# A decoder layer on one core: two quads with sums instead of three, a ring given back by halves, a new order of output and attention steps

## The chip, the cores and the metric

The kernel runs on one core of one Trainium2 chip. TensorE (PE) multiplies, VectorE (DVE) and ScalarE (ACT) work element by element, GpSimd (POOL) does next to nothing here, and SyncE (SP) issues the transfers. Times are microseconds. What counts is the device time of one execution; the figure given is the median of several.

## The reference

The program computes one layer of a decoder on x of 256 tokens by 2048 channels (f32), with RMSNorm ahead of each block:

```
x = x + 1/2 * SwiGLU_1(RMSNorm(x))
h = RMSNorm(x); h @ W_in -> conv B, C, x | pool p | q, k, v | 3 gates
x = x + W_out( sig(gA)*Wa(B*conv3(C*x)) + sig(gB)*Wb(pool(p)) + sig(gC)*Wc(attention(q,k,v)) )
x = x + 1/2 * SwiGLU_2(RMSNorm(x))
out = RMSNorm(x)
swiglu(h, w_in, w_out): a, b = split(h @ w_in); (silu(a) * b) @ w_out
```

The hidden width of each SwiGLU (FFN) is 5632. Attention has 8 heads of 128 over the 256 tokens, causal with a linear distance penalty.

## The kernel before

**Products.** Weights come from memory as f32 blocks of 128 x 512. ACT copies a block to a rounded `whi` (`high`, L236) and DVE forms the rest `wlo` (`low`, L240); the activations are kept in the same two parts. Every product is three matmuls of 512 columns: high x high, low x high, high x low (`three`). One transfer brings four blocks (1 MB, `emit_dma`, three buffers); one transfer is one *step*.

**Pairs.** In an FFN, 512 columns of a and the matching 512 of b are a *pair* (11 per FFN), computed in 8 quads of 256 input channels. In a plain quad ("P") four weight blocks meet four activation forms in 8 products. In a quad with sums ("S") a scheme with 7 products is used: DVE adds blocks in place (`block_sums`, L245 to L248), three blocks are used directly (kind "A") and the four summed blocks as kind "T". An S quad so has 21 matmuls and a P quad 24. `PATTERN` gives the kinds of a pair's quads; the first pair of each FFN is all P. The sums accumulate in eight PSUM banks K1 to K7 and K22. After the last S quad three early steps (`e1`, `e2`, `e3`) combine banks, one per half-step; after the last quad `evac` adds the rest, takes the sigmoid and multiplies: silu(a) * b as a token-major tile `gt`. Its two halves are transposed on PE later (`turn`), and split into gh and gl (L474, L475): the left side of the output products.

**Parts.** `PARTS = (3, 3, 2, 3)`: after so many pairs come their output chunks: four column chunks j, each of as many steps as the part has pairs (24 matmuls per step), added into the residual `xr` by `ev_o` (L500). With C steps next, the two `turn`s of the last pair are due 4 and 5 half-steps after its end. A step whose left side doesn't exist yet pops the waiting side work by force.

**Ring.** `whi` and `wlo` are a ring of `RING` blocks. `prepare(n)` takes blocks for the first kind of step n+1 and, where step n has sums, for its T blocks, and emits `high`, `block_sums` and `low`; `need(n)` says how many blocks must be free. `prepare_ahead` runs at each step's start as far as blocks are free; `release(n)` gives a step's blocks back when the step is emitted. Since each engine takes its instructions in the order in which they are emitted, this order decides who stands behind whom. From 12 steps before the end of the first FFN to the end of the mixer, blocks from `LEND` on are lent out as tiles ("units"), so the mixer has a ring of `LEND` blocks.

**Side work.** `later` puts closures into a queue with due half-steps; `lazy` ones (attention: `scores`, `transp`, `pv` for each head in turn) are popped one every two half-steps. The pool branch needs pool weights: at step `n_ffn1 - 2` they are issued (L867) and, right there, split by ACT and DVE (L869, L870).

**Start.** x0raw (x transposed) comes in four pieces j; `forms_xT` makes the forms of quads 2j and 2j+1. At steps 0, 2 and 4 it stands ahead of `prepare_ahead`. At steps 0 and 1 the last two pieces of x0raw and the two row blocks of x (1 MB each) are issued.

Of the kernel before, what the change touches and what calls it, by code (L numbers as in the profile page):

```python
# [26 lines left out]
PARTS = (3, 3, 2, 3)  # L27
PATTERN = "SPSPSPPP"
UNITS = 20
RAW_BUFS = 3  # L30
LOOK_DMA = 3
RING = 18
LEND = 10
DELAY = 3
# [8 lines left out]

K1, K2, K3, K4, K6, K7, K5, K22 = range(8)
NF = 8
# [13 lines left out]
def f32(ap):  # L59
    return ap.bitcast(F32)  # L60


@with_exitstack
def hybrid_trunk(ctx: ExitStack, tc: tile.TileContext, x, xT, wst, vecs, poolw, fnorm, consts, out):
# [76 lines left out]
    def wide(b):  # L141

        return bank[:, b:b + 2].rearrange("p b (k s) -> p (b k) s", s=S)

    def side_psum():

        at = steps[cur[0]]
        if at["kind"] != "C":
            assert not at["set"]["sums"]
            return wide(K6)  # L150
        return wide(take(4, 6) if at["far"] else 6)
# [22 lines left out]
    def pair(forms, pattern, early, evac):  # L174
# [102 lines left out]

    def prepare_ahead():
        while prepared[0] < len(steps) and need(prepared[0]) <= len(free):
            prepare(prepared[0])  # L280
            prepared[0] += 1

    def release(n):
        for a in steps[n]["items"]:
            free.extend(parts_t.pop((n, a)))
        reclaim()
        raw_t.pop(n, None)

# [131 lines left out]


    def in_set(n, xs, c, gs, pattern):

        t = {}
        pb = lambda k: bank[:, k]

        def e1():
            t["pu"], t["vw"] = tok_tile("pu"), tok_tile("vw")
            nc.scalar.activation(t["pu"][:, 0], pb(K1), AF.Copy)
            nc.vector.tensor_sub(t["pu"][:, 1], t["pu"][:, 0], pb(K6))  # L430

        def e2():
            u = t["pu"][:, 1:2].to_broadcast((P, 2, CH))
            nc.vector.tensor_add(t["vw"], bank[:, K7:K7 + 2], u)  # L434

        def e3():
            nc.vector.tensor_add(t["pu"][:, 1], t["vw"][:, 0], pb(K5))

        def evac():
            r = norm[n]  # L440
            if "S" in pattern:
                pu, vw = t["pu"], t["vw"]
                a = pu[:, 0], vw[:, 0]
                b = vw[:, 1], pu[:, 1]
# [4 lines left out]
            else:  # L449
                a, b = (pb(K2), pb(K4)), (pb(K3), pb(K22))  # L450
# [8 lines left out]
            if "S" in pattern:  # L459
                drop(t["pu"], t["vw"])  # L460
            if c == 10:
# [26 lines left out]
    def ffn(n, xs, after, first):  # L488
# [3 lines left out]
        for p, cnt in enumerate(PARTS):  # L492
# [82 lines left out]
    def ev_v(c):  # L575
# [8 lines left out]
        return ev  # L584

    def attention(h):
        slope = 2.0 ** (-(8.0 / H) * (h + 1))
# [46 lines left out]

        lazy.extend([scores, transp, pv])

# [181 lines left out]
    nc.scalar.activation(junk[:, :NT], mhalf, AF.Sigmoid)  # L818
    ps = wide(K6)
    for i in range(WARM):  # L820
# [41 lines left out]
    for n, g in enumerate(steps):  # L862
        cur[0] = n
        if n == n_ffn1 - 2:
            for c in range(2):
                raw = unit("pw", F32, (P, 2, 2, S))
                nc.sync.dma_start(raw, poolw[:, 2 * c:2 * c + 2])  # L867
                pw[c] = unit("pwh", F32R, (P, 2, 2, S)), unit("pwl", F32R, (P, 2, 2, S))
                nc.scalar.activation(pw[c][0], raw, AF.Copy)  # L869
                nc.vector.tensor_sub(pw[c][1], raw, f32(pw[c][0]))  # L870
                drop(raw)
            mx["inv"] = unit("inv", F32)
            nc.sync.dma_start(mx["inv"].rearrange("p g s -> p (g s)"), consts[:, C_INV:C_END])
# [22 lines left out]
        if n < tail_from:  # L896
            prepare_ahead()
        for half in range(2):
# [5 lines left out]
            while True:  # L904
                try:
# [153 lines left out]
```

## Time and profile before

| | |
|---|---|
| runs | 2343.77, 2345.73, 2346.03 us; median 2345.73 |
| profiled execution | 2341.46 us, its span 2339.7 us |
| PE busy | 2271.6 us, 97%, 10145 matmuls and transposes |
| DVE busy | 1542.9 us, 66% |
| ACT busy | 1050.7 us, 45% |
| DMA | 438.61 MB, mean 187 GB/s |
| mean granted clock of PE | 0.992 |

The shares are means over stages with different limits. Busy time of PE counts matmuls from start to modelled end, which overlap; the time between two starts is what a matmul costs. A granted clock of 1.00 is 2.4 GHz, 0.50 is 1.2 GHz.

### The profile page before, as it was taken

Reading aid. Unit: us, or ns where it says so; the run is one execution under the profiler, and the core shown is the slowest. Engines: PE = TensorE matmul, PEld = TensorE weight load, DVE = VectorE, ACT = ScalarE, POOL = GpSimd, SP = SyncE. Lnnn points to the kernel's source line nnn. Section 1 sums busy time; section 2 is a strip of 40 time slices with the busy share of each in tenths; the row PEclk is TensorE's granted clock in tenths of the full one; section 3 lists DMA queues with packets and bytes.
Section 4 is the critical chain, followed back from the end, with each engine's and each line's share of the span. In section 5 each row is a group of like instructions: output and inputs, shape, how many; then the busy total and the mean of one; then the engine's idle time right before and its main releaser. Section 6 shows DMA issues by size and latency. Waiting matters only on the chain.

```text
span 2339.7 us, 24296 instructions
## 1 busy us (share of the span) xinstructions
PE 2271.6 (97%) x10145; PEld 1866.5 (80%) x10145; DVE 1542.9 (66%) x1327; ACT 1050.7 (45%) x857; POOL 3.7 (0%) x9
## 2 busy tenths in 40 slices
PE   8999999999998999999999999999999999999998
PEld 6778788878877888888778888888878788878877
DVE  6976885867974565544544545556876885867975
ACT  6544453444444444444544334344544453444543
POOL 0000000000000000000000000000000000000000
PEclk9999999999999999999999999999999999999999
DMA  7464554455454545554445555545454554455453
GB/s 275 180 218 177 202 212 162 180 202 194 180 192 158 181 163 187 190 181 179 162 167 190 185 195 191 185 180 200 178 217 179 199 209 168 180 199 193 184 203 121
DMA packets 63470, 438.61 MB, mean 187 GB/s; under 512 B 7168, under 2 KB 7936, under 8 KB 11264
## 3 DMA queue, kind: packets, MB, share of 16 engines
q1 hardware_dynamic: 63360, 437.06, 51.2%
q8 instruction: 79, 1.29, 0.2%
q14 instruction: 31, 0.25, 0.0%
HBM read 434.94 MB, written 2.10 MB: 187 GB/s over the span
## 4 chain that ended last, share of the span: by engine, by line
PE 75%; DVE 17%; ACT 4%; issue 3%; DMA 1%; SPq 0%; POOLq 0%; ACTq 0%; DVEq 0%
PE bank L310 49%; PE bank L299 24%; DVE wlo L240 9%; ACT whi L236 3%; DVE gt L456 1%; PE bank L377 1%; DVE raw L246 1%; DVE raw L247 1%; DVE raw L245 1%; DVE vw L434 1%; DVE gl L475 0%; DMA pw<-poolw_dram 0%; DMA x0raw<-xT_dram 0%; DVE pu L445 0%; DVE pu L448 0%
## 5 line engine op out<-in xcount | busy, mean ns | idle before, releaser
L240 DVE TENSOR_TENSOR wlo<-raw,whi 128x2048 fp32r<-128x2048 f32 (+2 forms) x483 | 1031.0, 2157 | 650.3 <-ACT whi L236 649.0
L236 ACT ACTIVATE whi<-raw 128x2048 fp32r<-128x2048 f32 (+2 forms) x483 | 865.4, 1807 | 974.4 <-PE bank L310 501.9
L299 PE MATMUL bank<-whi,fhl 128*128 128x512 f32 x1760 | 563.0, 393 | 5.1 <-ACT whi L236 5.1
L299 PEld LDWEIGHTS bank<-whi,fhl 128*128 128x128 f32 x1760 | 332.2, 189 | 73.7 <-ACT whi L236 5.6
L299 PE MATMUL bank<-wlo,fhl 128*128 128x512 f32 x880 | 344.4, 391 | 1.6 <-DVE wlo L240 1.5
L310 PE MATMUL bank<-whi 128*128 128x512 f32 x752 | 297.5, 396 | 6.0 <-ACT whi L236 6.0
L310 PE MATMUL bank<-wlo,whi 128*128 128x512 f32 x752 | 294.6, 392 | 3.2 <-DVE wlo L240 3.1
L310 PE MATMUL bank<-whi,wlo 128*128 128x512 f32 x752 | 294.2, 391 | 1.3 <-DVE wlo L475 1.3
L310 PE MATMUL bank<-whi,gl 128*128 128x512 f32 (+1 forms) x684 | 267.4, 391 | 10.1 <-DVE gl L475 10.1
L310 PE MATMUL bank<-whi,gh 128*128 128x512 f32 (+1 forms) x684 | 267.8, 391 | 3.3 <-ACT gh L474 3.3
L310 PE MATMUL bank<-wlo,gh 128*128 128x512 f32 (+1 forms) x684 | 266.0, 389 | 0.0
L299 PE MATMUL bank<-wlo,fh 128*128 128x512 f32 x468 | 184.1, 393 | 18.5 <-DVE wlo L240 18.5
L299 PEld LDWEIGHTS bank<-wlo,fhl 128*128 128x128 f32 x880 | 166.1, 189 | 36.2 <-DVE wlo L240 2.5
L299 PE MATMUL bank<-whi,fh 128*128 128x512 f32 x468 | 183.3, 392 | 1.9 <-ACT whi L236 1.6
L299 PE MATMUL bank<-whi,fl 128*128 128x512 f32 x468 | 182.5, 390 | 0.0
L310 PEld LDWEIGHTS bank<-whi 128*128 128x128 f32 x752 | 141.9, 189 | 35.0 <-ACT whi L236 6.4
L310 PEld LDWEIGHTS bank<-wlo,whi 128*128 128x128 f32 x752 | 141.8, 189 | 34.9 <-DVE wlo L240 6.3
L310 PEld LDWEIGHTS bank<-whi,wlo 128*128 128x128 f32 x752 | 141.7, 188 | 31.1 <-DVE wlo L475 1.8
L310 PEld LDWEIGHTS bank<-whi,gl 128*128 128x128 f32 x684 | 129.9, 190 | 39.3 <-DVE gl L475 13.1
L310 PEld LDWEIGHTS bank<-whi,gh 128*128 128x128 f32 x684 | 130.1, 190 | 29.2 <-ACT gh L474 3.8
L310 PEld LDWEIGHTS bank<-wlo,gh 128*128 128x128 f32 x684 | 130.0, 190 | 26.0
L299 PEld LDWEIGHTS bank<-wlo,fh 128*128 128x128 f32 x468 | 87.9, 188 | 41.9 <-DVE wlo L240 24.1
(198 smaller groups left out, 1846.8 us busy)
## 6 DMA issues: line engine op xcount, KB each, us to landing
raw<-w_dram SPq DMA_DIRECT2D x405, 1024.0 KB, 4.8
raw<-w_dram SPq DMA_DIRECT2D x8, 256.0 KB, 4.7
xr<-x_dram SPq DMA_DIRECT2D x2, 1024.0 KB, 10.6
out_dram<-xr SPq DMA_DIRECT2D x8, 256.0 KB, 3.0
x0raw<-xT_dram SPq DMA_DIRECT2D x3, 512.0 KB, 7.6
raw<-w_dram SPq DMA_DIRECT2D x2, 512.0 KB, 8.2
pw<-poolw_dram SPq DMA_DIRECT2D x2, 512.0 KB, 7.8
fn<-fnorm_dram SPq DMA_DIRECT2D x2, 512.0 KB, 6.9
```

The source lines that it names most:

```text
L236: nc.scalar.activation(whi[:, b:b + c], raw_t[n][:, i:i + c], AF.Copy)
L240: nc.vector.tensor_sub(wlo[:, b:b + c], raw_t[n][:, i:i + c], f32(whi[:, b:b + c]))
L245: nc.vector.tensor_add(r[:, 0], r[:, 0], r[:, 3])
L246: nc.vector.tensor_add(r[:, 3], r[:, 3], r[:, 2])
L247: nc.vector.tensor_add(r[:, 2], r[:, 2], r[:, 0])
L299: nc.tensor.matmul(bank[:, k], a, b, start=e["start"][at + j] and i == 0, stop=e["stop"][at + j] and i == 2)
L310: nc.tensor.matmul(acc[t], a, w[:, cols], start=g["first"] and k == 0 and i == 0, stop=g["last"] and k == KG - 1 and i == 2)
L377: nc.tensor.transpose(ps[:, i, t * P:(t + 1) * P], src(t, k), idn)
L434: nc.vector.tensor_add(t["vw"], bank[:, K7:K7 + 2], u)
L456: nc.vector.scalar_tensor_tensor(gt[:, i], o[i], r[:, i:i + 1], gt[:, i], op0=ALU.mult, op1=ALU.mult)
```

## The change

- `PATTERN` has S quads at 0 and 4 only. Within the S quad at 4 all four T products come first, then the three A products; `release` can so give the T blocks back after its first half.
- `release(n, half)` gives blocks back after each half-step; `prepare_ahead` also runs in the middle of a step. The ring has 20 blocks (12 kept by the mixer, 10 before); there are 17 units for 20.
- The banks have a new order, so that K2, K4 and K3, K22 are adjacent. A fixed tile `ev` takes the place of two units. `evac` adds two banks at a time and multiplies two halves at a time; the factor r moves from there into `half_r2` (0.5 r^2), used in `ev_o` and `finish`.
- `out_order`: in the first two output chunks of a part the last pair's steps come after all others of both chunks. The order of the weights in memory follows.
- Attention: `scores` of head i, then `transp` of head i-1, then `pv` of head i-2.
- Pool weights: issued at `n_ffn1 - 4`, split at `n_ffn1 + 3`.
- Start: the blocks of step 1 are cut singly and those of step 2 by twos; at step 0 only two steps are prepared; `forms_xT` stands behind `prepare_ahead`.

```diff
-PATTERN = "SPSPSPPP"
-UNITS = 20
+PATTERN = "SPPPSPPP"
+UNITS = 17
-RING = 18
-LEND = 10
+RING = 20
+LEND = 12
-K1, K2, K3, K4, K6, K7, K5, K22 = range(8)
+K1, K6, K2, K4, K7, K5, K3, K22 = range(8)
+def out_order(cnt):
+    return [c * cnt + i for c in range(2) for i in range(cnt - 1)] + [c * cnt + cnt - 1 for c in range(2)]
...
-                mm = [[("A", 1, A12, K2), ("T", 0, F5, K5), ("T", 3, F7, K7), ("T", 2, F6, K6)],
-                      [("T", 1, A22, K4), ("A", 2, F3, K3), ("A", 0, A11, K1)]]
+                mm = [[("T", 0, F5, K5), ("T", 3, F7, K7), ("T", 2, F6, K6), ("T", 1, A22, K4)],
+                      [("A", 1, A12, K2), ("A", 2, F3, K3), ("A", 0, A11, K1)]]
                 if q == 0:
-                    mm = [mm[0][1:] + mm[1][2:], mm[0][:1] + mm[1][:2]]
+                    mm[0][3], mm[1] = mm[1][2], [mm[0][3]] + mm[1][:2]
...
     def prepare(n):
         a = first_of(n + 1)
         ra = ring(n + 1, a, SIZE[a]) if a else ()
+        if n < 2:
+            ra = [(i + x, b + x, 2 >> (1 - n)) for i, b, c in ra for x in range(0, c, 2 >> (1 - n))]
...
-    def prepare_ahead():
-        while prepared[0] < len(steps) and need(prepared[0]) <= len(free):
+    def prepare_ahead(most=None):
+        while prepared[0] < (most or len(steps)) and need(prepared[0]) <= len(free):
...
-    def release(n):
-        for a in steps[n]["items"]:
-            free.extend(parts_t.pop((n, a)))
+    def release(n, half):
+        e = steps[n]
+        if e["kind"] == "C":
+            done = {"W": slice(2 * half, 2 * half + 2)}
+        else:
+            rest = {m[0] for m in e["mm"][1]} if half == 0 else ()
+            done = {a: slice(0, 4) for a in e["items"] if a not in rest and (n, a, 0) not in gone}
+            if e["kind"] == "P":
+                used = sorted({m[1] for m in e["mm"][half]})
+                assert used in ([0, 1], [2, 3])
+                done = {"W": slice(used[0], used[0] + 2)}
+        for a, sl in done.items():
+            if (n, a, half) not in gone:
+                gone.add((n, a, half))
+                free.extend(parts_t[n, a][sl])
...
         def evac():
             r = norm[n]
+            a, b = bank[:, K2:K2 + 2], bank[:, K3:K3 + 2]
             if "S" in pattern:
-                nc.vector.tensor_add(a[0], pb(K2), a[0])
-                nc.vector.tensor_add(a[1], pb(K4), a[1])
-                nc.vector.tensor_sub(b[0], pb(K3), b[0])
-                nc.vector.tensor_sub(b[1], pb(K22), b[1])
+                nc.vector.tensor_add(ev[:, 0:2], a, ev[:, 0:2])
+                nc.vector.tensor_sub(ev[:, 2:4], b, ev[:, 2:4])
+                a, b = ev[:, 0:2], ev[:, 2:4]
             gt = tok_tile("gt")
             for i in range(NT):
-                nc.scalar.activation(gt[:, i], a[i], AF.Sigmoid, scale=r[:, i:i + 1])
-            for o in (a, b):
-                for i in range(NT):
-                    nc.vector.scalar_tensor_tensor(gt[:, i], o[i], r[:, i:i + 1], gt[:, i],
-                                                   op0=ALU.mult, op1=ALU.mult)
+                nc.scalar.activation(gt[:, i], a[:, i], AF.Sigmoid, scale=r[:, i:i + 1])
+            nc.vector.tensor_mul(gt, a, gt)
+            nc.vector.tensor_mul(gt, b, gt)
...
-                        nc.vector.scalar_tensor_tensor(xv, acc[:, t], 0.5, xv, op0=ALU.mult, op1=ALU.add)
+                        nc.vector.scalar_tensor_tensor(xv, acc[:, t], half_r2(n)[:, t:t + 1], xv, op0=ALU.mult, op1=ALU.add)
...
+            mine = steps[-4 * cnt:]
+            steps[-4 * cnt:] = [mine[i] for i in out_order(cnt)] + mine[2 * cnt:]
...
-        lazy.extend([scores, transp, pv])
+        stages[h] = [scores, transp, pv]
+        if h == H - 1:
+            for i in range(H + 2):
+                lazy.extend(stages[i - k][k] for k in range(3) if 0 <= i - k < H)
...
-        if n == n_ffn1 - 2:
+        if n == n_ffn1 - 4:
             for c in range(2):
-                raw = unit("pw", F32, (P, 2, 2, S))
-                nc.sync.dma_start(raw, poolw[:, 2 * c:2 * c + 2])
+                pw[c] = unit("pw", F32, (P, 2, 2, S))
+                nc.sync.dma_start(pw[c], poolw[:, 2 * c:2 * c + 2])
...
+        if n == n_ffn1 + 3:
+            for c in range(2):
+                raw = pw[c]
                 pw[c] = unit("pwh", F32R, (P, 2, 2, S)), unit("pwl", F32R, (P, 2, 2, S))
                 nc.scalar.activation(pw[c][0], raw, AF.Copy)
                 nc.vector.tensor_sub(pw[c][1], raw, f32(pw[c][0]))
...
-        if n in (0, 2, 4):
-            forms_xT(n // 2 + 1)
...
         if n < tail_from:
-            prepare_ahead()
+            prepare_ahead(2 if n == 0 else None)
+        if n in (0, 2, 4):
+            forms_xT(n // 2 + 1)
...
+            if half and n < tail_from and n:
+                prepare_ahead()
             if g["kind"] != "C":
                 emit_pair(n, half)
+                release(n, half)
                 continue
...
-        if not g.get("tail"):
-            release(n)
```

## Rows read from the trace of the kernel before

**Rows 1.** The page's first part: busy time (share of the span) and instructions.
```profile
PE 2271.6 (97%) x10145; PEld 1866.5 (80%) x10145; DVE 1542.9 (66%) x1327; ACT 1050.7 (45%) x857; POOL 3.7 (0%) x9
```
**Rows 2.** Stage table: stretch, length, busy and count per engine, clock, DMA, GB/s.
```profile
170.00:250.00 80.00, 80.00 (x354) 66.29 (x354) 51.42 (x38) 33.44 (x20) 0.00 (x0) 1.00 0.50 176
250.00:330.00 80.00, 76.80 (x340) 62.77 (x340) 72.98 (x68) 38.31 (x28) 0.00 (x0) 1.00 0.50 190
```
**Rows 3.** Waits of PE: line, releaser, total us, times, longest.
```profile
PE bank L299 <- DVE wlo L240: 20.1, 16, 1.9
PE bank L310 <- DVE gl L475: 10.1, 7, 1.7
...
PE bank L310 <- ACT whi L236: 6.0, 1, 6.0
PE bank L613 <- DVE e L605: 6.0, 8, 1.2
PE bank L310 <- DVE wlo L240: 4.4, 7, 1.5
PE bank L310 <- ACT gh L474: 3.3, 2, 1.7
PE bank L310 <- DVE wlo L475: 1.3, 1, 1.3
```
**Rows 4.** Groups by line and form: count, busy us, mean ns, idle before.
```profile
L299 PE MATMUL bank<-wlo,fh 128*128 128x512 f32 x468 | 184.1, 393 | 18.5 <-DVE wlo L240 18.5
...
L240 DVE TENSOR_TENSOR wlo<-raw,whi 128x2048 fp32r<-128x2048 f32 x405 | 922.2, 2290 | 643.9 <-ACT whi L236 642.6
L240 DVE TENSOR_TENSOR wlo<-raw,whi 128x1536 fp32r<-128x1536 f32 x52 | 91.1, 1752 | 5.4 <-ACT whi L236 5.4
...
L456 DVE SCALAR_TENSOR_TENSOR gt<-pu,rstd,gt 128x512 f32<-128x512 f32 x40 | 29.8, 744 | 0.0
...
L434 DVE TENSOR_TENSOR vw<-bank,pu 128x1024 f32<-128x1024 f32 x20 | 24.5, 1224 | 0.7
```
**Rows 5.** Timeline at a second quad with sums: start, us, engine, operation.
```profile
111.20 0.68 DVE L245 TENSOR_TENSOR raw<-raw 128x512 f32<-128x512 f32 x1
...
113.98 6.15 DVE L240 TENSOR_TENSOR wlo<-raw,whi 128x2048 fp32r<-128x2048 f32 x3
...
118.52 0.50 PE L299 MATMUL bank<-wlo,fh 128*128 128x512 f32 x1 [1.86 <-DVE wlo L240]
118.85 0.39 PE L299 MATMUL bank<-whi,fl 128*128 128x512 f32 x1
```
**Rows 6.** Timeline and stage table at the output of a part of two pairs.
```profile
509.42 0.50 PE L310 MATMUL bank<-whi,gh 128*128 128x512 f32 x1 [1.66 <-ACT gh L474]
...
511.86 0.79 PE L310 MATMUL bank<-whi,gl 128*128 128x512 f32 x1 [1.71 <-DVE gl L475]
...
510.91:517.74 6.83, 5.88 (x14) 4.62 (x15) 1.49 (x3) 0.00 (x0) 0.00 (x0) 0.50 0.55 209
```
**Rows 7.** Timeline of ACT at the pool weights, and the stage table there.
```profile
749.71 1.06 ACT L869 ACTIVATE whi<-pw 128x1024 fp32r<-128x1024 f32 x1 [9.98 <-DMA pw<-poolw_dram]
...
753.26:760.09 6.83, 4.41 (x10) 3.13 (x11) 4.34 (x6) 3.86 (x6) 0.00 (x0) 0.50 0.37 127
```
**Rows 8.** Timeline of PE at one head's transposes.
```profile
1132.98 0.33 PE L613 MATMUL bank<-idn,e 128*128 128x128 f32 x1 [0.67 <-DVE e L605]
```
**Rows 9.** Timeline of the start, and the stage table there.
```profile
12.26 0.39 PE L299 MATMUL bank<-whi,fl 128*128 128x512 f32 x1
14.22 0.91 ACT L355 ACTIVATE fh<-x0raw,vec 128x256 fp32r<-128x256 f32 x2 [3.68 <-DMA x0raw<-xT_dram]
...
25.59 1.91 ACT L236 ACTIVATE whi<-raw 128x2048 fp32r<-128x2048 f32 x1 [4.26 <-DMA raw<-w_dram]
...
28.33 0.39 PE L299 MATMUL bank<-whi,fh 128*128 128x512 f32 x1
...
15.98:26.22 10.24, 6.91 (x15) 5.07 (x16) 7.16 (x5) 5.97 (x4) 0.00 (x0) 0.50 1.02 408
```

More of the change, by code (lines that the diff above doesn't have):

```diff
@@ L81, in hybrid_trunk @@
     bank = pp.tile([P, 8, CH], F32, name="bank")
+    ev = cp.tile([P, 4, CH], F32, name="ev")
     pw = {}
@@ L149, in side_psum @@
             assert not at["set"]["sums"]
-            return wide(K6)
+            return wide(K7)
         return wide(take(4, 6) if at["far"] else 6)
@@ L276, in prepare @@
             emit_dma(n + 1 + LOOK_DMA)
-    def prepare_ahead():
-        while prepared[0] < len(steps) and need(prepared[0]) <= len(free):
+    def prepare_ahead(most=None):
+        while prepared[0] < (most or len(steps)) and need(prepared[0]) <= len(free):
             prepare(prepared[0])
             prepared[0] += 1
-    def release(n):
-        for a in steps[n]["items"]:
-            free.extend(parts_t.pop((n, a)))
+    def release(n, half):
[13 more added lines that the diff above has]
+                free.extend(parts_t[n, a][sl])
         reclaim()
-        raw_t.pop(n, None)
+        if half:
+            raw_t.pop(n, None)
+    gone = set()
     def three(ah, al, b):
@@ L418, in x_side, with half_r2 @@
         return go
+    def half_r2(n):
+        if ("h", n) not in norm:
+            norm["h", n] = sp.tile([P, NT], F32, tag="hr", name="hr")
+            nc.vector.scalar_tensor_tensor(norm["h", n], norm[n], 0.5, norm[n], op0=ALU.mult, op1=ALU.mult)
+        return norm["h", n]
     def in_set(n, xs, c, gs, pattern):
-        t = {}
-        pb = lambda k: bank[:, k]
         def e1():
-            t["pu"], t["vw"] = tok_tile("pu"), tok_tile("vw")
-            nc.scalar.activation(t["pu"][:, 0], pb(K1), AF.Copy)
-            nc.vector.tensor_sub(t["pu"][:, 1], t["pu"][:, 0], pb(K6))
+            nc.scalar.activation(ev[:, 0], bank[:, K1], AF.Copy)
+            nc.vector.tensor_sub(ev[:, 3], ev[:, 0], bank[:, K6])
@@ L432, in e2 @@
         def e2():
-            u = t["pu"][:, 1:2].to_broadcast((P, 2, CH))
-            nc.vector.tensor_add(t["vw"], bank[:, K7:K7 + 2], u)
+            nc.vector.tensor_add(ev[:, 1:3], bank[:, K7:K7 + 2], ev[:, 3:4].to_broadcast((P, 2, CH)))
         def e3():
-            nc.vector.tensor_add(t["pu"][:, 1], t["vw"][:, 0], pb(K5))
+            nc.vector.tensor_add(ev[:, 3], ev[:, 1], bank[:, K5])
         def evac():
             r = norm[n]
+            a, b = bank[:, K2:K2 + 2], bank[:, K3:K3 + 2]
@@ L441, in evac @@
             if "S" in pattern:
-                pu, vw = t["pu"], t["vw"]
-                a = pu[:, 0], vw[:, 0]
-                b = vw[:, 1], pu[:, 1]
-                nc.vector.tensor_add(a[0], pb(K2), a[0])
-                nc.vector.tensor_add(a[1], pb(K4), a[1])
-                nc.vector.tensor_sub(b[0], pb(K3), b[0])
-                nc.vector.tensor_sub(b[1], pb(K22), b[1])
-            else:
-                a, b = (pb(K2), pb(K4)), (pb(K3), pb(K22))
+                nc.vector.tensor_add(ev[:, 0:2], a, ev[:, 0:2])
@@ L459, in evac @@
-            if "S" in pattern:
-                drop(t["pu"], t["vw"])
+                nc.scalar.activation(gt[:, i], a[:, i], AF.Sigmoid, scale=r[:, i:i + 1])
+            nc.vector.tensor_mul(gt, a, gt)
+            nc.vector.tensor_mul(gt, b, gt)
             if c == 10:
@@ L584, in ev_v @@
         return ev
+    stages = {}
     def attention(h):
@@ L818, in hybrid_trunk @@
     nc.scalar.activation(junk[:, :NT], mhalf, AF.Sigmoid)
-    ps = wide(K6)
+    ps = wide(K7)
     for i in range(WARM):
@@ L863, in hybrid_trunk @@
         cur[0] = n
-        if n == n_ffn1 - 2:
+        if n == n_ffn1 - 4:
             for c in range(2):
-                raw = unit("pw", F32, (P, 2, 2, S))
-                nc.sync.dma_start(raw, poolw[:, 2 * c:2 * c + 2])
+                pw[c] = unit("pw", F32, (P, 2, 2, S))
+                nc.sync.dma_start(pw[c], poolw[:, 2 * c:2 * c + 2])
+            mx["inv"] = unit("inv", F32)
+            nc.sync.dma_start(mx["inv"].rearrange("p g s -> p (g s)"), consts[:, C_INV:C_END])
+        if n == n_ffn1 + 3:
+            for c in range(2):
+                raw = pw[c]
                 pw[c] = unit("pwh", F32R, (P, 2, 2, S)), unit("pwl", F32R, (P, 2, 2, S))
@@ L871, in hybrid_trunk @@
                 drop(raw)
-            mx["inv"] = unit("inv", F32)
-            nc.sync.dma_start(mx["inv"].rearrange("p g s -> p (g s)"), consts[:, C_INV:C_END])
         if n in (0, 1):
@@ L925, in hybrid_trunk @@
                 emit_mm(n, range(2 * half, 2 * half + 2), range(NT), {t: acc[:, t] for t in range(NT)})
-        if not g.get("tail"):
-            release(n)
+                release(n, half)
         if g["last"] and g["evac"]:
@@ L936, in finish @@
         xv = xr[:, t, j * CH + c0:j * CH + c1]
-        nc.vector.scalar_tensor_tensor(xv, o, 0.5, xv, op0=ALU.mult, op1=ALU.add)
+        nc.vector.scalar_tensor_tensor(xv, o, half_r2(2)[:, t:t + 1], xv, op0=ALU.mult, op1=ALU.add)
         junk = sp.tile([P, CH], F32, tag="junk", name="junk", bufs=1)
@@ L1020 @@
                     order.append((wi[:, c * CH:(c + 1) * CH], wi[:, FF + c * CH:FF + (c + 1) * CH]))
-                order.append(wo[c0 * CH:(c0 + cnt) * CH])
+                mine = [wo[(c0 + i) * CH:(c0 + i + 1) * CH, j * CH:(j + 1) * CH] for j in range(4) for i in range(cnt)]
+                order += [mine[i] for i in out_order(cnt)] + mine[2 * cnt:]
                 c0 += cnt
```

## The prediction

> **What bounds the kernel now.** I read the busy shares first, then a table of stages, then the waits of the tensor engine, then the stretches around its longest waits. TensorE (PE) is busy 97% of the span, VectorE (DVE) 66%, ScalarE (ACT) 45% [rows 1]. In an output stage PE starts 354 matmuls in 80.00 us without a gap, so one matmul of 512 columns takes 0.226 us from start to start, and that pitch is the price of every matmul here; one stage on, among the pairs, PE is busy 76.80 of 80 and DVE 72.98 [rows 2]. So there are two ways to get faster: fewer matmuls, or fewer waits of PE. The change pays for the second with more of the first.
>
> The waits of PE that I use sum to 51 us [rows 3]. A wait costs 0.27 more than its row shows: 0.17 because back-to-back matmuls overlap (0.39 long, 0.226 apart) [rows 4], and 0.1 because the matmul after it follows at 0.33, not 0.226 [rows 5].
>
> **More products.** A quad with sums has 7 products of 3 matmuls, a plain one 8 of 3. Twenty pairs have sums (all but the first of each FFN); in each one quad turns plain: 20 x 3 x 0.226 = **+13.6 us** of PE, hidden by nothing. The Trainium skill (TensorE: Matmul & The Clock Gate, "Back-to-back issue gap") gives about 216 ns for an isolated gap at 512 columns and about 131 ns sustained; by these the term would be 12.9 or 7.9. The measured pitch decides, so the page's lower figure gets no chance of its own.
>
> **Waits at quads with sums.** DVE work of one pair now [rows 4, 5]: low parts 5 x 2.290 + 3 x (1.752 + 2.290) = 23.6; block sums 12 x 0.68 = 8.2; early steps e1 to e3 0.68 + 1.22 + 0.68 = 2.6 (1.22 for a whole tile); ending 4 x 0.68 + 4 x 0.744 = 5.7; gl 2 x 0.68 = 1.4 (0.68 is the price of half a tile in the block sums). Sum 41.5, against PE's 183 x 0.226 = 41.4 and about 1 of transposes. DVE is as full as PE there. The wait comes at the second quad with sums (q2). With 18 blocks, after q0 leaves, 4 (q1) and 3 (q2's direct blocks) are held; the next cut needs 4 + 4 and fits only at the start of q1, one quad (5.4 us) ahead. It takes 4 x 0.68 + 2.29 + 2.29 = 7.3 us of DVE. The rows show it: sums from 111.20, three lows from 113.98, PE waiting 1.86 until 118.52 [rows 5].
>
> After the change, with sums at q0 and q4 and 20 blocks: 19 are held when q0 starts, 15 after it with q4's direct blocks, 11 after q1, so the cut for q4's sums (8 blocks) starts at q2, two quads (10.9 us) ahead for the same 7.3 us; the next q0's likewise at q6. DVE per pair becomes 6 x 2.290 + 2 x 4.042 = 21.8, sums 5.4, early 2.6, ending 4 x 1.22 = 4.9, gl 1.4: 36.1 against PE's 186 x 0.226 + 1 = 43. I let these waits go: 18.5 idle in the wlo,fh group, of which 0.2 is at the start of the kernel, and 14 x 0.27 = **-22.1** [rows 3, 4]. The cover is 3.6 us of slack per cut. Against it: at q4 the summed blocks now come first, with no product of a direct block (0.7 us) before them. Should all waits stay, the term is 0. Next late at such a quad is the ending's second addition (1.22 after the last matmul); its banks are written again only in the second half of q0, 2.7 us in, so it costs nothing.
>
> Edits that cost nothing: half_r2 is one small operation per FFN, and an AP for an immediate in 62 output evacuations costs at most 0.744 - 0.68 each, 4 us of DVE beside full PE work. Cutting ring blocks in more runs costs DVE (4 x 0.68 - 2.29) / 3 = 0.14 per run; one more in every quad is 1.1 of the 7 us free per pair, and that much per pair without this cover.
>
> **Output order.** Each part's first output chunk waits for the transposes of the last pair, popped 4 and 5 half-steps after it. With three pairs the tile is used in the third step, at once; with two pairs (PARTS has one 2) it is forced in the second: PE waits 1.66 and 1.71 close together, and then runs 6.83 us at a granted clock of 0.50, the lower of its two levels (1.2 of 2.4 GHz) [rows 6]. In the new order the tile is used two steps later (three pairs) or one step later (two pairs). In the second case its second half is popped in the step that uses it, half a step (2.7 us) ahead, and behind a weight cut on ACT (1.91) and DVE (2.29), so its low half ends 1.91 + 2.29 + 0.68 = 4.9 into the step and is wanted at about 3.7 (2.7, 0.5 of transposes, 0.45 to the third matmul): 1.2 late, 2.5 for both FFNs. The rest goes: gl 10.1 + gh 3.3 + the one with gl in a lent block 1.3 = 14.7, plus 10 x 0.27, plus two clock losses of 6.83/2 = 3.4, less 2.5: **-21.7** [rows 3, 6].
>
> **Pool weights.** ACT stood 9.98 us for the pool weights' transfer, with the next step's high part behind it; PE waited 6.0, then ran 6.83 us at half clock [rows 3, 7]. Now the transfer is issued two steps earlier and read seven steps after that, some 38 us; the copies lie in a step of the mixer where DVE has room. 6.0 + 0.27 + 3.4 = **-9.7**. What is late next, the last transposed piece of x1, is popped two steps before its use.
>
> **Attention and mixer.** The transposes of each head wait up to 0.67 for the softmax that began one step earlier, 8 times [rows 3, 8]. With the stages of three heads interleaved the gap is two or three pops, over 10 us, for a chain of one step and 0.67: 6.0 + 8 x 0.1 = **-6.8**. The ring that the mixer keeps grows from 10 to 12 blocks (three whole steps, not two), so cuts start a step earlier: 4.4 + 7 x 0.27 = **-6.3** [rows 3]. From the other side these two give 0, if another releaser stands right behind.
>
> **The start.** Here an edit works against itself. PE now stops after the matmul of 12.26, since ACT first waits for x0raw until 14.22 and makes forms ahead of step 1's blocks; step 2 starts at 28.33, after a stretch at half clock [rows 9]. After the change step 1's blocks are cut singly and first, and it can run from 12.5 to 17.9; step 2's blocks (landing at 14.22 + 1.05 MB / 0.408 = 16.8) and forms come about 1.2 late, it ends at 24.6, step 3 at 30.0. But the forms of step 4 now stand behind the preparation of four more steps, the last being step 6's, and ACT takes them in order (before, they stood between step 4's and step 5's blocks). The DMA engines are full in this stretch (share 1.02, 408 GB/s), and step 4's block landed at 25.59 [rows 9]. After it come step 5's (1.05 MB), x0raw (0.52), the second row block of x (1.05) and step 6's own 1.05: 3.67 MB / 0.408 = 9.0 us, so 34.6. Then 1.9 for the high part, 2.29 for the low one, which stands ahead of the forms on DVE, and 0.5: the third matmul of step 4 runs at about 39.3, and the step ends at 44.3. Now it ends at 28.33 + 3 x 5.44 = 44.65. The wait of some 9 us can bring a half-clock stretch as at 15.98: 0 to 5.1 lost (10.24 / 2), of which most falls into the wait; I take 1.5. In sum **+1**; from both sides -9 (no wait at step 4) to +6.
>
> **Sum.** 13.6 - 22.1 - 21.7 - 9.7 - 6.8 - 6.3 + 1 = -52.0. The profiled execution took 2341.46 us (span 2339.7), so 2289.5. The median of the runs shown, 2345.73, is 4.3 above it: **2294**.
>
> **The rivals.** (1) *The start gains.* If nothing holds step 6's block back, steps 0 to 4 run with 1 to 2 us of waits and the start gives -9: 2284. For it: step 1 does begin 5 us earlier; against it: the full DMA engines. (2) *The waits at quads with sums move to q0 and q4 instead of going*: 22.1 stay, 2316. For it: the summed blocks come first and a cut still needs 7.3 us of DVE; against: it begins one quad earlier and DVE has 7 us free per pair. (3) *Slower*: the same place, but at every quad with sums. ACT and DVE are in order, and with the ring given back by halves the plain cuts are queued ahead of the pair's ending, so the cut for the sums comes over 3.6 us late each time; 40 quads at the present mean wait of 1.58 (22.1 / 14) cost 63. Without the 22.1 saved, that is 2294 + 22.1 + 63 = 2379; it decides from (52.0 - 22.1) / 40 = 0.75 us per quad on. For it only that DVE was full; against: 36.1 of 43. (4) *Another releaser stands right behind half of the waits in the mixer and the outputs*: about half of 21.7 + 6.8 + 6.3, +17, 2311.
>
> **How the numbers follow.** The forecast has 0.58, (1) 0.20, (2) 0.08, (3) 0.04, (4) 0.10. The likeliest case by itself spans 2288 to 2303. Range **2279 to 2316**: down to the start's gain with some small waits that I did not count, up to (2) and (4). Faster by over 0.2% (4.7 us, about what a measurement of this kernel can tell from no change) 0.95, within 0.2% 0.02, slower 0.03: only (3), or several terms failing together, reach that.
>
> **What would show it.** In the changed profile: 60 matmuls more in the pairs' line; no PE wait over 0.5 us at q0 and q4 of the middle pairs; PE waits on gl and gh all but gone, and no half clock near 510, 750 and 2090; no ACT wait on the pool weights; no PE wait at the softmax transposes; DVE under 90% among pairs; and at the start PE busy from 12.5 to 30, then idle until about 37 while ACT waits for a weight block. The prediction is wrong if waits above 0.75 us stand at most quads with sums, or if the pitch of a matmul is not 0.226.

## The result, and the profile after

The changed kernel takes 2288.31 us (median of 4, 2287.95 to 2289.06) where the kernel before took 2344.75 beside it: ratio 0.976, interval 0.9743 to 0.9777. The forecast was 2294; 4.3 of the 5.7 us between them is the distance of the traced execution before (2341.46) from its median, which the forecast added, and which the changed kernel doesn't have (2288.16 traced). The profiled execution has a span of 2286.4 for 2339.7.

The first part of the page after (beside [rows 1]): PE has 60 matmuls more and is 8.5 us less busy, since busy time counts overlaps and half clock too; its share is 99%.

```profile
span 2286.4 us, 24602 instructions
PE 2263.1 (99%) x10205; PEld 1873.3 (82%) x10205; DVE 1459.9 (64%) x1271; ACT 1035.4 (45%) x967; POOL 3.7 (0%) x9
```

All waits of PE in the changed kernel (line, releaser, total us, times, longest; beside [rows 3]). L323 is the pairs' line, L334 that of the steps, L401 the transposes. Of the 51 us read before, 0.2 is left at a weight cut; gl, gh, the pool weights' block and the softmax are gone. What stands there now is new: 6.8 for forms (L379), 2.5 for transposes (L366) and 1.4 for an evacuation (L808).

```profile
PE bank L323 <- ACT fh L379: 6.8, 1, 6.8
PE bank L401 <- DVE wlo L366: 2.5, 2, 1.7
PE bank L323 <- DVE xr L808: 1.4, 1, 1.4
PE bank L323 <- ACT whi L242: 1.2, 1, 1.2
PE bank L845 <- DVE mhalf L840: 1.2, 1, 1.2
PE bank L323 <- DVE fl L380: 1.1, 1, 1.1
PE bank L323 <- DVE fhl L380: 0.5, 1, 0.5
PE bank L323 <- ACT fhl L379: 0.4, 1, 0.4
PE bank L323 <- DVE wlo L246: 0.2, 1, 0.2
```

The stage table after, an output stage and a stage of pairs (beside [rows 2]): PE is busy 80.00 of 80 in both, and DVE among pairs 64.35 where it had 72.98. The third row is the only low-clock stretch left before the end.

```profile
155.00:235.00 80.00, 80.00 (x358) 66.27 (x357) 47.88 (x38) 29.82 (x20) 0.00 (x0) 1.00 0.50 179
230.00:310.00 80.00, 80.00 (x359) 66.24 (x358) 64.35 (x51) 37.50 (x29) 0.00 (x0) 1.00 0.55 202
34.79:45.03 10.24, 7.06 (x16) 5.09 (x17) 8.52 (x9) 10.18 (x18) 0.00 (x0) 0.50 0.74 266
```

Where the time went, counted from the start of each stage's first matmul in both traces (after minus before; the terms of the prediction beside it):

| stages | measured | predicted |
|---|---|---|
| pairs with sums, both FFNs | -11.4 (13.6 of products, so -25.0 of waits) | 13.6 - 22.1 |
| output chunks, with the end at the pool weights | -30.7 | -21.7 - 9.7 |
| mixer, gates with attention, W_out, first pair of FFN 2 | -13.6 (2.9, 8.7, 1.4, 0.6) | -6.8 - 6.3 |
| start, up to the first quad with sums | +2.4 | +1 |
| sum | -53.3 | -52.0 |

The start after (timeline of ACT, then PE and DVE; beside [rows 9]). PE runs to 29.69, and then has no forms: ACT waits 4.66 for step 6's block, cuts it from 34.50, and only then makes the forms; the third matmul comes at 39.19. The prediction had 34.6, about 37 and 39.3.

```profile
27.92 1.92 ACT L242 ACTIVATE whi<-raw 128x2048 fp32r<-128x2048 f32 x1 [0.66 <-DMA raw<-w_dram]
34.50 1.91 ACT L242 ACTIVATE whi<-raw 128x2048 fp32r<-128x2048 f32 x1 [4.66 <-DMA raw<-w_dram]
36.32 0.89 ACT L379 ACTIVATE fh<-x0raw,vec 128x256 fp32r<-128x256 f32 x2
...
29.69 0.39 PE L323 MATMUL bank<-whi,fhl 128*128 128x512 f32 x1
36.86 0.79 PE L323 MATMUL bank<-whi,fh 128*128 128x512 f32 x1 [6.79 <-ACT fh L379]
...
39.19 0.79 PE L323 MATMUL bank<-whi,fl 128*128 128x512 f32 x1 [1.11 <-DVE fl L380]
...
36.44 2.29 DVE L246 TENSOR_TENSOR wlo<-raw,whi 128x2048 fp32r<-128x2048 f32 x1 [4.28 <-ACT whi L242]
38.65 0.88 DVE L380 SCALAR_TENSOR_TENSOR fl<-x0raw,vec,fh 128x256 fp32r<-128x256 f32 x2
```

One wait is new and was not in the prediction. With both first chunks of a part ending together, the transposes of two chunks for the mixer come one step apart, and share one pair of PSUM banks. Timeline of PE at 710 in the changed kernel: the second set waits for DVE to have read the first. It costs 2.8 with its restart.

```profile
710.32 0.66 PE L401 MATMUL bank<-idn,xr 128*128 128x128 f32 x4 [1.70 <-DVE wlo L366]
711.74 0.66 PE L401 MATMUL bank<-idn,xr 128*128 128x128 f32 x4 [0.76 <-DVE wlo L366]
```

### The profile page after: what moved, and what is told of

It is laid out like the page before. It is cut to its first block, busy times and chain, and to the rows that moved or that the text cites. A ratio compares the mean times of both kernels' runs of the same rounds, so it can differ in the third digit from the quotient of the medians.

```text
span 2286.4 us, 24602 instructions
## 1 busy us (share of the span) xinstructions
PE 2263.1 (99%) x10205; PEld 1873.3 (82%) x10205; DVE 1459.9 (64%) x1271; ACT 1035.4 (45%) x967; POOL 3.7 (0%) x9
## 4 chain that ended last, share of the span: by engine, by line
PE 97%; DMA 1%; ACT 1%; DVE 1%; issue 0%; SPq 0%; POOLq 0%; DVEq 0%; ACTq 0%
PE bank L334 55%; PE bank L323 40%; PE bank L401 1%; DMA raw<-w_dram 1%; ACT whi L242 0%; PE bank L747 0%; DVE wlo L246 0%; DMA x0raw<-xT_dram 0%; PE bank L615 0%; PE bank L645 0%; ACT junk L411 0%; DVE wlo L366 0%; PE bank L646 0%; PE bank L614 0%; PE bank L580 0%
## 5 line engine op out<-in xcount | busy, mean ns | idle before, releaser
L246 DVE TENSOR_TENSOR wlo<-raw,whi 128x1536 fp32r<-128x1536 f32 (+2 forms) x597 | 1009.5, 1721 | 665.8 <-ACT whi L242 664.8
L242 ACT ACTIVATE whi<-raw 128x1536 fp32r<-128x1536 f32 (+2 forms) x597 | 851.4, 1455 | 929.8 <-PE bank L334 417.6
L323 PE MATMUL bank<-whi,fhl 128*128 128x512 f32 x2112 | 665.4, 391 | 1.0 <-DVE fhl L380 0.5
L323 PEld LDWEIGHTS bank<-whi,fhl 128*128 128x128 f32 x2112 | 396.4, 188 | 83.4 <-DVE fhl L380 1.0
L323 PE MATMUL bank<-wlo,fhl 128*128 128x512 f32 x1056 | 411.1, 389 | 0.0
L334 PE MATMUL bank<-whi 128*128 128x512 f32 x896 | 352.6, 394 | 0.0
L334 PE MATMUL bank<-whi,wlo 128*128 128x512 f32 x896 | 349.0, 390 | 0.0
L334 PE MATMUL bank<-wlo,whi 128*128 128x512 f32 x896 | 348.7, 389 | 0.0
L334 PE MATMUL bank<-whi,gh 128*128 128x512 f32 (+1 forms) x684 | 265.3, 388 | 0.0
L334 PE MATMUL bank<-whi,gl 128*128 128x512 f32 (+1 forms) x684 | 263.8, 386 | 0.0
L334 PE MATMUL bank<-wlo,gh 128*128 128x512 f32 (+1 forms) x684 | 263.7, 386 | 0.0
L323 PEld LDWEIGHTS bank<-wlo,fhl 128*128 128x128 f32 x1056 | 198.4, 188 | 40.4
L334 PEld LDWEIGHTS bank<-whi,wlo 128*128 128x128 f32 x896 | 168.2, 188 | 35.3
L334 PEld LDWEIGHTS bank<-wlo,whi 128*128 128x128 f32 x896 | 168.3, 188 | 34.2
L334 PEld LDWEIGHTS bank<-whi 128*128 128x128 f32 x896 | 168.3, 188 | 33.8
L334 PEld LDWEIGHTS bank<-whi,gl 128*128 128x128 f32 x684 | 128.5, 188 | 25.9
L334 PEld LDWEIGHTS bank<-wlo,gh 128*128 128x128 f32 x684 | 128.6, 188 | 25.3
L334 PEld LDWEIGHTS bank<-whi,gh 128*128 128x128 f32 x684 | 128.6, 188 | 25.1
L323 PE MATMUL bank<-whi,fh 128*128 128x512 f32 x312 | 123.0, 394 | 9.4 <-ACT fh L379 6.8
L323 PE MATMUL bank<-whi,fl 128*128 128x512 f32 x312 | 122.8, 394 | 1.1 <-DVE fl L380 1.1
L323 PE MATMUL bank<-wlo,fh 128*128 128x512 f32 x312 | 122.7, 393 | 0.2 <-DVE wlo L246 0.2
```

The lines of the kernel that those rows point to most:

```text
L242: nc.scalar.activation(whi[:, b:b + c], raw_t[n][:, i:i + c], AF.Copy)
L246: nc.vector.tensor_sub(wlo[:, b:b + c], raw_t[n][:, i:i + c], f32(whi[:, b:b + c]))
L323: nc.tensor.matmul(bank[:, k], a, b, start=e["start"][at + j] and i == 0, stop=e["stop"][at + j] and i == 2)
L334: nc.tensor.matmul(acc[t], a, w[:, cols], start=g["first"] and k == 0 and i == 0, stop=g["last"] and k == KG - 1 and i == 2)
```

## The experiments

Each ran beside the kernel before, whose median was between 2340.5 and 2343.2 in these series, some us lower than above; so differences of 1 or 2 us between series say nothing by themselves, and where it matters the traces are compared stage by stage. The start varies too: five kernels that have the changed kernel's start reach the first quad with sums between 62.6 and 64.4 us.

### Two sums alone, in the kernel before

```diff
-PATTERN = "SPSPSPPP"
+PATTERN = "SPPPSPPP"
```

> The kernel before with sums at quads 0 and 4 and nothing else changed. Theory A (a cut for sums fits the ring of 18 only one quad ahead, 5.4 us for 7.3 us of DVE): the waits stay, now at quad 4 and quad 0, and 13.6 us of matmuls come on top: 2350 to 2375. Theory B (the wait was the pair's ending standing ahead of the cut on DVE, and quad 4 has no ending near it): the waits go even with 18 blocks, 13.6 - 22: 2336.

Measured 2319.79, ratio 0.9907 (0.9878 to 0.9936). Theory B, and better than it said: no wait at a quad with sums is left in the pairs (the stages of pairs take exactly as long as in the changed kernel, within 0.1 us), with 18 blocks, whole release and the long ending. Theory A, which was the prediction's reason, falls. Timeline of DVE in this kernel, at the quad that began at 278.46: the long ending is over at 260.9, the sums run at 267.03, ahead of their place in the ring's order, because they need raw blocks and not ring blocks (the cut of the summed blocks on ACT had to wait for PE to free the ring, until 273.27); the low part of the sums is done at 277.51, one us before the quad begins.

```profile
260.17 0.75 DVE L456 SCALAR_TENSOR_TENSOR gt<-pu,rstd,gt 128x512 f32<-128x512 f32 x1
...
267.03 0.69 DVE L245 TENSOR_TENSOR raw<-raw 128x512 f32<-128x512 f32 x1
...
270.14 2.29 DVE L240 TENSOR_TENSOR wlo<-raw,whi 128x2048 fp32r<-128x2048 f32 x1 [0.24 <-ACT whi L236]
275.22 2.29 DVE L240 TENSOR_TENSOR wlo<-raw,whi 128x2048 fp32r<-128x2048 f32 x1 [2.79 <-ACT whi L236]
```

In the changed kernel the same low parts end at 274.91 for a quad that begins at 279.03: its edits together bought 3 us more margin there, and no time.

```profile
268.41 0.69 DVE L254 TENSOR_TENSOR raw<-raw 128x512 f32<-128x512 f32 x1
270.35 4.56 DVE L246 TENSOR_TENSOR wlo<-raw,whi 128x2048 fp32r<-128x2048 f32 x3 [1.25 <-ACT whi L242]
```

This kernel also lost 9.6 us of waits at the two outputs of two pairs (4.7 and 4.9, from the stage starts), with the output order untouched: gh and gl come 0.25 and 1.14 late there, not 1.66 and 1.71, and the half-clock stretches of [rows 6] are gone. That they come earlier because DVE is no longer behind is likely, but no run shows it by itself. In all, the pattern alone takes 21.3 of the 53.3 us between the traces.

### Three sums with everything else changed

```diff
-PATTERN = "SPPPSPPP"
-UNITS = 17
+PATTERN = "SPSPSPPP"
+UNITS = 19
-RING = 20
-LEND = 12
+RING = 18
+LEND = 10
```

> The changed kernel with sums at quads 0, 2 and 4 as before, on a ring of 18 blocks (10 in the mixer) and 19 units, since 20 blocks and three pairs of forms don't fit; halves given back, shorter ending and all orders as changed. Theory (DVE was as full as PE, and the cut one quad ahead is late): 13.6 us of matmuls go, the 22 of waits at quad 2 come back, as many or more as the summed products come first now: 2297 to 2305. Rival (the halves and the shorter ending had removed the waits, and the third quad with sums was given up for nothing): 2275.

Measured 2295.30, ratio 0.9802 (0.9774 to 0.9831): the theory, at the low end of its range, and the rival falls. The waits are back at quad 2 although the summed products, the halves and the short ending are as changed. Waits of PE in the pairs, then DVE and PE at one quad 2: sums at 263.22 to 266.1, right behind the ending; four low parts until 272.2; PE waits 1.05.

```profile
PE bank L323 <- DVE wlo L246: 14.0, 23, 1.8
```

```profile
262.08 1.23 DVE L476 TENSOR_TENSOR gt<-ev,gt 128x1024 f32<-128x1024 f32 x1
263.22 0.68 DVE L251 TENSOR_TENSOR raw<-raw 128x512 f32<-128x512 f32 x1
...
266.00 6.22 DVE L246 TENSOR_TENSOR wlo<-raw,whi 128x2048 fp32r<-128x2048 f32 x4
...
270.55 0.50 PE L323 MATMUL bank<-wlo,fh 128*128 128x512 f32 x1 [1.05 <-DVE wlo L246]
```

So a third quad with sums is worth 13.6 us of PE and costs more than that in waits. How much more depends on the rest: the run with 18 blocks and two sums (next) differs from this one in pattern and units alone, and is 4.6 us faster (3.3 between the traces); in the kernel before, the same step gave 21.3.

### The ring undone: 18 blocks, then 18 blocks and whole release

```diff
-RING = 20
-LEND = 12
+RING = 18
+LEND = 10
```

> The changed kernel with a ring of 18 blocks for 20 and 10 kept by the mixer for 12; all else as changed. Theory (DVE full of work was the cause of the waits at quads with sums, as the kernel before with two sums showed without a larger ring): none there; only the mixer loses, whose waits of 4.4 us in 7 places cost 6.3 with their restart: 2293 to 2295. Rival (the ring carries the gain in the pairs): over 10 us more, 2300.

Measured 2290.74, ratio 0.9778 (0.9758 to 0.9798). No waits on weight cuts in the mixer (W_in takes 0.4 us less than in the changed kernel, the gates the same), and at most 1.0 per part in the pairs, 3.0 in all outside the start's aftermath. W_out and the first pair of FFN 2 take 3.0 more, half of it a longer wait for the last evacuation of W_out (2.8 for 1.4, first row below), while the start and the transposes of 710 take less. Both expectations are off: where halves are given back, the ring's size is worth about 3 us, and none of it in the mixer's weight cuts.

```profile
PE bank L323 <- DVE xr L808: 2.8, 1, 2.8
PE bank L401 <- DVE wlo L366: 1.0, 2, 0.8
```

```diff
     def release(n, half):
+        if half == 0:
+            return
+        for a in e["items"]:
+            free.extend(parts_t[n, a])
...
```

> The changed kernel with the whole ring part undone: 18 blocks, 10 in the mixer, a step's blocks given back at the step's end and so cut at step starts only. With 18 blocks and halves there was no wait left in the pairs and in the mixer. Theory (halves are what the mixer's waits needed; the pairs need neither, by DVE's room): seven waits on weight cuts in the mixer come back, 6.3 more than the 2290.7 of 18 blocks: 2297, no waits at quads with sums. Rival (each of ring and halves is idle, the mixer's waits went by the pool weights' or another edit): 2291.

Measured 2297.77, ratio 0.9811 (0.9791 to 0.9831): the theory. The mixer's waits on weight cuts are back (L341 is the steps' line here), and two on gl, one in each part of two pairs; the pairs have none after the start. The total is the expected one partly by luck: against the run with 18 blocks and halves the mixer takes 5.8 us more, the two parts of two pairs 3.3, which nobody expected, and the chunk ahead of the mixer 1.5, while the pairs and the first pair of FFN 2 take 4.6 less.

```profile
PE bank L341 <- DVE wlo L246: 3.4, 9, 0.8
PE bank L341 <- DVE gl L499: 2.7, 2, 1.3
```

### The output order undone

```diff
-    return [c * cnt + i for c in range(2) for i in range(cnt - 1)] + [c * cnt + cnt - 1 for c in range(2)]
+    return list(range(2 * cnt))
```

> The changed kernel with the steps of the output chunks (and the weights in memory) in the old order. Theory by the kernel before with two sums (the order alone, once DVE has room: its waits on gl and gh were 9.0 + 0.5 + 1.3 us in 10 places and brought no half clock): 10.8 + 10 x 0.27 = 13.5 more, 2302. Rival (my term as predicted, with two half-clock stretches): 21.7 more, 2310.

Measured 2294.08, ratio 0.9792 (0.9773 to 0.9812): 5.8 more, less than either. By stages the output chunks lose 10.0 (1.6, 4.3 and 4.1 in three of the eight parts, with half-clock stretches in the two of two pairs), and 2.9 come back at the transposes of 710, which are then a chunk apart again. Five parts of three pairs lose nothing; in the kernel before with two sums, also in the old order, such a part takes 1.6 more (67.86 for 66.23). That cuts in mid-step make the difference is likely, but no run has that edit alone in the old order.

### The pool weights at the old place

```diff
-        if n == n_ffn1 - 4:
+        if n == n_ffn1 - 2:
...
-        if n == n_ffn1 + 3:
+        if n == n_ffn1 - 2:
```

> The changed kernel with the pool weights issued and split at the old place, two steps before the mixer. Theory: ACT stands for the transfer with a weight block behind it, PE waits some 6 us and runs 6.83 us at half clock: 9.7 more, 2298. Rival (20 blocks and cuts in half-steps have put more blocks ahead of that place, so a wait of ACT is covered): under 4 more, 2292 or less.

Measured 2293.45, ratio 0.979 (0.977 to 0.9809): between the two, 4.2 by stages. ACT stands nearly as long as before (9.23 for 9.98), but the step that PE is in has its blocks; the block behind the copies comes 1.83 late, with a half-clock stretch of 3.4 after it.

```profile
736.76 1.06 ACT L898 ACTIVATE whi<-pw 128x1024 fp32r<-128x1024 f32 x1 [9.23 <-DMA pw<-poolw_dram]
...
743.34 0.50 PE L334 MATMUL bank<-wlo,whi 128*128 128x512 f32 x1 [1.83 <-DVE wlo L246]
```

### Attention in the old order, and the old ending

```diff
-        if h == H - 1:
-            for i in range(H + 2):
-                lazy.extend(stages[i - k][k] for k in range(3) if 0 <= i - k < H)
+        lazy.extend(stages[h])
```

> The changed kernel with the attention stages of the heads one after the other, as before. Theory (the transposes start one step after their head's scores, too early for the softmax chain): eight waits of 0.67 to 1.2 come back, 6.0 + 8 x 0.1 = 6.8 more, 2295. Rival (the larger ring and the cuts in half-steps had taken ACT and DVE work out of that chain's way): under 3 more.

Measured 2291.38, ratio 0.9784 (0.9764 to 0.9803). The stage with attention takes 2.1 us more (the start 1.0, which varies from run to run): the rival. One wait of eight is left.

```profile
PE bank L634 <- DVE e L626: 0.9, 1, 0.9
```

```diff
-                nc.vector.tensor_add(ev[:, 0:2], a, ev[:, 0:2])
+                for i in range(NT):
+                    nc.vector.tensor_add(ev[:, i], a[:, i], ev[:, i])
...
-            nc.vector.tensor_mul(gt, a, gt)
+            for o in (a, b):
+                for i in range(NT):
+                    nc.vector.scalar_tensor_tensor(gt[:, i], o[:, i], r[:, i:i + 1], gt[:, i], op0=ALU.mult, op1=ALU.mult)
```

> The changed kernel with the pair's ending as before: four additions of half a tile, and four multiplications with r of half a tile (the output's factor is then 0.5 alone). Theory (DVE has 7 us free per pair): 5.7 for 4.9 of DVE per pair, beside PE: 2288, no change. Rival (the ending on DVE was what held the cut for sums back, and its shortening is part of the gain): waits of PE at quads 0 or 4 in most pairs, 5 to 20 more.

Measured 2289.07, ratio 0.9774 (0.9754 to 0.9793). Every stage from the first quad with sums to the end takes what it takes in the changed kernel, within 0.1 us; the start 0.4 more. The short ending is hidden, as the prediction had it.

### The start

```diff
+        if n in (2, 4):
+            forms_xT(n // 2 + 1)
         if n < tail_from:
             prepare_ahead(2 if n == 0 else None)
-        if n in (0, 2, 4):
-            forms_xT(n // 2 + 1)
+        if n == 0:
+            forms_xT(1)
```

> The changed kernel with the forms of quads 4 to 7 put ahead of the preparation again at steps 2 and 4 (at step 0 they stay behind it). Theory (ACT and DVE take the forms of quad 4 behind the blocks of later steps): the forms now stand behind step 5's block only, whose high part ran from 27.92 to 29.8 and whose low part ends at about 32.1, so the third matmul of step 4 runs at about 32.6 and not 39.19; 6.6 us less, and up to 2.2 more if the half-clock stretch goes: 2280 to 2282. Rival (what PE waits for there is the transfer of x0raw, or the full DMA engines whatever the order): no change, 2288.

```diff
+        if n in (1, 3):
+            forms_xT(n // 2 + 2)
         if n < tail_from:
             prepare_ahead(2 if n == 0 else None)
-        if n in (0, 2, 4):
-            forms_xT(n // 2 + 1)
+        if n == 0:
+            forms_xT(1)
```

> The changed kernel with the forms of quads 4 and 5 made at step 1 and those of quads 6 and 7 at step 3, each ahead of that step's preparation. Theory (order on ACT and DVE): x0raw for them landed by about 20.5, so they run at about 20 and step 4 waits for nothing; the whole wait of 6.8 + 1.1 and the half-clock stretch after it go: 11 to 12 us less, 2277. Rival (the DMA engines set the pace of the start): step 6's block still lands at 34.5, but that is 6 us ahead of its use, so a loss would show as a wait for a weight block at steps 4 to 7; 2283 or more.

Measured 2286.85 (ratio 0.9766, 0.9738 to 0.9795) and 2287.26 (0.9768, 0.974 to 0.9796): both expectations of a gain fall. Of the wait at step 4, 1.9 and 1.6 are left in the first, nothing in the second, but PE waits further on instead, at the first quad with sums. Timeline of PE in the second kernel:

```profile
57.20 0.70 PE L323 MATMUL bank<-whi,fh 128*128 128x512 f32 x1 [3.42 <-ACT whi L242]
59.61 0.79 PE L323 MATMUL bank<-wlo,fh 128*128 128x512 f32 x1 [1.70 <-DVE wlo L246]
```

Behind step 6's block (here at 35.78, after ACT waited 5.67 for it) ACT has cuts, forms, sums of forms and squares in one row until the summed blocks of step 8 are cut at 57.15. In the changed kernel that cut ends no earlier, at 57.46, but PE, held up at step 4, gets there at 63.35 and finds it done. Two kernels shorten it:

```diff
-        later(x_side(1, j, x1))
+        later(x_side(1, j, x1), delay=5 if j == 1 else None)
...
-        if SQ <= n < SQ + 4:
-            squares(None, ssq[0], pieces[2 * (n - SQ):2 * (n - SQ + 1)])
-        if n == 7:
+        if n in (2, 4):
+            squares(None, ssq[0], pieces[2 * n - 4:2 * n])
+        if n == 5:
             norm[0] = rstd_of(ssq[0])
-        if 5 <= n < 8:
-            for q in range(8)[n - 5::3]:
+        if n == 3:
+            forms_xT(3)
+        if n in (2, 9):
+            for q in (0 if n == 2 else 4,):
...
-        if n == 8:
+        if n == 10:
             drop(*x0raw.values())
...
-        if n < tail_from:
-            prepare_ahead(2 if n == 0 else None)
-        if n in (0, 2, 4):
-            forms_xT(n // 2 + 1)
+        if n in (0, 1):
+            prepare_ahead(n + 2)
+            forms_xT(n + 1)
+        if 0 < n < tail_from:
+            prepare_ahead()
```

The diff is that of the second; the first has the forms of quads 6 and 7 at step 2, the squares at steps 2, 5 and 6, the norm at 7, and the sums of quad 4's forms at step 4.

> The changed kernel with the start put in another order: the forms of quads 4 and 5 behind step 3's block only, and, while ACT waits for step 6's block, the forms of quads 6 and 7, the sums of quad 0's forms and four of the eight squares; the other sums at step 4, the other squares at steps 5 and 6. In addition the transposes of the second output chunk of the last part two half-steps later. Theory (the start is a chain on ACT that begins when step 6's block lands at 34 to 36, with some 22 us of cuts, forms, sums and squares before the summed blocks of step 8 are ready): 5 to 7 us of that chain move into the idle stretch before it, and a wait of 2.7 us at the chunk goes: 2278 to 2281. Rival (the DMA engines set the pace, whatever ACT does): only the 2.7 us, 2285.

> The start once more: squares at steps 2 and 4, the norm at step 5, forms of quads 6 and 7 at step 3, the sums of quad 4's forms at step 9 (they are wanted at step 12). Theory (the chain ahead of step 8's summed blocks on ACT and DVE sets the end of the start; it had waits of 1.6, 1.1 and 5.6 left at steps 6 to 8): 2.6 us of sums and up to 3 of the norm's way leave that chain, some 4 us less than 2282.2: 2278. Rival (what is left is the summed blocks' own cut, 7 us from the moment the ring has room): 2281 to 2282.

Measured 2282.16 (ratio 0.974, 0.9724 to 0.9756) and **2277.33** (ratio 0.9725, 0.9708 to 0.9741), the fastest kernel here: against the changed one 11.2 us less up to the first quad with sums, 3.1 more right behind it, 2.9 less at the transposes of 710. The summed blocks of step 8 still come late in it, after a wait of 1.89, and no stretch at half clock is left before the end:

```profile
54.49 0.50 PE L323 MATMUL bank<-wlo,fh 128*128 128x512 f32 x1 [1.89 <-DVE wlo L246]
57.82 0.50 PE L323 MATMUL bank<-whi,fh 128*128 128x512 f32 x1 [0.56 <-DVE gt L475]
```

## Why the prediction was right

**Total and sign.** It rested on PE being the bound at 0.226 us per matmul and on its waits having nothing behind them. Both held: the predicted sum was -52.0, the traces differ by 53.3, and after the start PE has no wait among the pairs but the one at the start of FFN 2. That nothing stood behind the waits was more than the prediction could know, since it allowed for other releasers (its fourth rival). The closeness of the sum is partly luck: single terms are off by up to 2.9, in both directions.

**Waits at quads with sums.** Size right (-22.1 predicted, -25.0 measured), reason wrong. The step that failed is the walk through the ring, which made the start of a cut in the program its start in time. In the runs the engines run ahead of the order of emission as far as their own waits allow: the block sums need no ring block, and with two quads with sums DVE did them at 267.03, some 6 us before the ring let the cut in. Two sums alone removed the waits with 18 blocks and whole release, so neither a larger ring nor halves were needed for it, and three sums on the changed kernel brought them back. Two readings of that remain: DVE has less to do per pair (41.5 us by the prediction's count, now 36.1), or quad 4 lies further from the pair's ending than quad 2 did. In the kernel before, the waits stood at quad 2 and not at quad 4, which speaks for the place; sums at quads 0 and 2 would tell them apart, and were not run. The prediction's second rival, that the waits move to q4 and q0, has nothing in its favour in the middle pairs of the changed kernel.

**Outputs.** Predicted -21.7, measured about -23.4 (the -30.7 less the pool weights' 10.1, and without the new wait of 2.8). The 2.5 kept for the two parts of two pairs did not come: at 507 PE goes from the transposes into the products without a wait. Giving blocks back by halves took it away: with 18 blocks and halves there is none either, and with whole release gl comes 1.34 late in both parts, close to the 1.2 predicted (row below). But the term is shared: two sums alone took 9.6 of it, undoing the order costs only 10.0, and which other edit freed most of the parts of three pairs is not shown.

```profile
511.68 0.50 PE L341 MATMUL bank<-whi,gl 128*128 128x512 f32 x1 [1.34 <-DVE gl L499]
```

**Pool weights, attention, mixer.** -9.7 measured as 10.1; -13.1 as 13.6. Again the sizes hold and the single causes don't: undone alone, pool weights cost 4.2 and the order of attention 2.1. The second sum hides two misses, too: the stage with attention gained 8.7 where 6.8 were counted, the rest of the mixer 4.9 where 6.3 were; the longest of the seven waits counted there (1.5, at 756.48) stands in the output chunk behind the pool weights. The prediction also has the softmax waits as up to 0.67; the longest is 1.2 [rows 3], and their sum, which it used, is right. As to the mixer's cause: with 10 blocks and halves there are no waits on weight cuts, with 10 blocks and whole release nine. So halves are enough, and the larger ring, which the prediction named, isn't needed; whether 12 blocks with whole release would have been enough as well was not run.

**The start.** Right in place and time, to 0.1 us at step 6's block. It came out at +2.4 for +1: from 39.19 on 14 matmuls at half clock took 6.0 us where 3.2 are the price at full clock, a loss of 2.8 for the 1.5 assumed. The experiments on it add what the prediction did not see: the wait at step 4 was the visible part of a longer chain on ACT, so the same chain's other end was late when it was taken away.

**Left out.** The new wait of 2.8 at the transposes of 710, from the moved output steps, and a wait of 1.4 at the start of FFN 2 (L808 in the list of waits), where the new order of banks makes the first product wait for the last evacuation of W_out.

## What to carry to other kernels

Price a wait at what PE loses from start to start, and sum the waits before asking what removes them; here that sum held to 1.3 us, with single terms off by up to 2.9. Which edit removes them is another question: where several edits each give the same side engine room, the gains don't add, and only one-at-a-time runs in both directions (one part alone, one part undone) tell them apart. When a wait is removed at the start of a chain in order, look along that chain for the next place that was hidden behind it.

## What the runs showed of the hardware

Between 14 and 27 us of the changed kernel the 16 DMA engines moved 422 GB/s, at a busy share of 1.02 (row below); the share stays at 1.01 or more until ACT can start on step 6's block at 34.50. In the two kernels that only moved forms ahead, ACT waits for that transfer until 35.78 and 36.35, so the transfers, not ACT's order, set when it arrives.

```profile
14.00:27.00 13.00, 12.03 (x53) 9.32 (x52) 6.44 (x8) 7.19 (x8) 0.00 (x0) 1.00 1.02 422
```

Cutting blocks in smaller runs was free here: 597 low parts, 149 of them of one block, for 459 in the kernel before with two sums cost DVE about 21 us (138 x 0.15; one more run costs (4 x 0.685 - 2.291) / 3 by the rows below). No stage shows it: with whole release and 463 low parts, the pairs (128.37 us for three) and the output chunks of three pairs (66.23) take the same time.

```profile
L246 DVE TENSOR_TENSOR wlo<-raw,whi 128x2048 fp32r<-128x2048 f32 x264 | 603.9, 2291 | 528.8 <-ACT whi L242 528.5
L246 DVE TENSOR_TENSOR wlo<-raw,whi 128x1536 fp32r<-128x1536 f32 x179 | 314.2, 1756 | 132.9 <-ACT whi L242 132.3
L246 DVE TENSOR_TENSOR wlo<-raw,whi 128x512 fp32r<-128x512 f32 x149 | 102.0, 685 | 1.7 <-ACT whi L242 1.6
```
